# A hybrid decoder trunk: the spread inverse softmax sums in another buffer ring, and one small transpose in another PSUM bank

## The chip, the cores and the metric

The kernel runs on one core of one Trainium2 chip. The metric is the device time of one execution in microseconds (us); the median of three runs before the change is 1223.66 us (1223.54 to 1223.89). In the profile the engines are PE (TensorE, matrix products), PEld (its weight loads), DVE (VectorE), ACT (ScalarE), POOL (GpSimd) and SP (SyncE, which issues all transfers of this kernel, in order).

## The reference

Two layers over a sequence of 1024 tokens of width 1024. Each projects its input, runs a main branch and a memory attention, gates both, projects back and normalises. The main branch of the second layer is a forgetting attention with 16 heads of width 64, and the change lies there:

```python
logits = jnp.einsum('bqhd,bkhd->bhqk', qi, k) * scale
logits = logits + (ci[..., :, None] - cum_k[:, :, None, :])
logits = jnp.where(mask[None, None], logits, -jnp.inf)
p = jax.nn.softmax(logits, axis=-1)
return jnp.einsum('bhqk,bkhd->bqhd', p.astype(v.dtype), v)
...
y = jnp.concatenate([y_main * jax.nn.silu(g_main), y_mem * jax.nn.silu(g_mem)], axis=-1)
return y @ w_out
```

The kernel does not divide by the softmax's sums at once. It multiplies the unnormalised probabilities by the values and divides the output of a pair of heads afterwards, by a product with the inverse sums.

## The kernel before

**Heads and pairs.** The function `fox` runs over the 16 heads, two to a pair (`pr` is 0 to 7, `b` is 0 or 1 within it), and for each head over eight row blocks of 128 queries (step `i`, from the longest block, 1024 keys, to the shortest, 128). A last, shorter round (`hd == HEADS`) finishes what is left. Into these steps it mixes dense projections (`slab`, L253), which are to keep PE busy: keys, queries, values and gates of later pairs, and at the end the first part of the output projection (L498).

**One row block.** In `probs`, POOL writes the causal mask into the forget row R (`affine_select`, L881). It can do so only when DVE has read R for the block before. PE makes the logits in one of three banks "L" (L231). DVE adds R and finds the row's extreme (L889), for long blocks in two parts; the second part contains the masked columns. ACT takes the exponentials into one of two banks "T" and adds up their sums (L895), then writes their high half as float16 into a buffer of the ring "P" (L902). DVE writes the low half beside it (`halves`, L909), one step later. `turn` transposes the buffer by a transfer (L941), after which the buffer is free again. Five steps later (`LAG`) PE multiplies with the values (L958, L964) into the single bank "O", and ACT and DVE move the result out (L970, L971), which frees that bank.

**The inverse sums of a pair.** They are made in the round after the pair's second head, so those of pair `pr - 1` while pair `pr` runs; "in pair 6" below means then. At step 2 `inverse_rows` adds and inverts the sums on DVE, PE turns them with one small transpose (L920) into bank "O", ACT copies the result (L921), and SP writes it to DRAM (L922). At step 3 `inverse_wide` takes a buffer of 128x1024 and loads each head's inverse sums into 64 of its partitions (L944; in the last round L929). `pair_out` multiplies the pair's output by it in four pieces on POOL (L981). For most pairs POOL multiplies each piece with the gate as well (L983); pairs 3, 5 and 6 get their gate later, in `late_gate`. Then the output goes to DRAM (`y1d`, L985). The output projection reads `y1d` back (L529), splits it into a high and a low part (L187 on ACT, L188 on DVE) and multiplies (L498).

**Rings.** A ring is a number of equal buffers under one name; a new tile takes one whose former owner is done, and its first writer waits for that. "P" has four buffers. The probabilities of a row block use them, and before the change the spread inverse sums too; later the norm's two vectors (L517) and part of one output weight do. "V" has four: the turned values of a pair, and in the last pair and after it the high and low parts of two output weights (numbers 1 and 9 of `wtags`, L1092).

**What sets the order.** PE's instructions stand in the order in which the code writes them. The other engines' orders are set by a scheduler when the kernel is built, and each engine runs its own in order. One that waits holds everything behind it on its engine.

Of the kernel before, what the change touches and what calls it, by code (L numbers as in the profile page):

```python
# [9 lines left out]
F32 = mybir.dt.float32  # L10
# [8 lines left out]
P = 128  # L19
S = 1024  # L20
D = 1024
KT = D // P
ST = S // P
NH = 512
# [75 lines left out]
def trunk_kernel(ctx, tc, x, xT, memT, win, wk, wv0, wv, wmk, wmv, wout, poolw, pscale, lng, lnb, bforget, out):  # L100
# [21 lines left out]
    def nm(tag):  # L122
        count[0] += 1
        return f"{tag}{count[0]}"

    def sb(shape, tag, bufs, dt=F32, where=None):
        return (where or pool).tile(shape, dt, tag=tag, name=nm(tag), bufs=bufs)

    def ps(shape, tag, bufs):
        return psum.tile(shape, F32, tag=tag, name=nm(tag), bufs=bufs)  # L130
# [554 lines left out]
    with tc.tile_pool(name="in1", bufs=1) as in1:  # L685
# [7 lines left out]
        def vt(shape, dt=F32R):  # L693
            return sb(shape, "V", 4, dt, in1)
# [219 lines left out]
        def inverse_rows(pr, sums, rows):  # L914

            r = sums[:, 0]
            nc.vector.tensor_tensor(r, sums[:, 0], sums[:, 1], ALU.add)
            nc.vector.reciprocal(r, r)
            t = ps([P, NH], "O", 1)[: 2 * ST, :P]
            nc.tensor.transpose(t, r.rearrange("p b i -> p (b i)"), ident)  # L920
            nc.scalar.copy(rows, t)  # L921
            nc.sync.dma_start(inverses[pr], rows)  # L922

        def inverse_wide(pr):

            wide = sb([P, S], "P", 4)
            for b in range(2):
                load = wide[64 * b : 64 * b + 64], inverses[pr, ST * b : ST * b + ST].rearrange("i q -> (i q)").partition_broadcast(64)
                due.append(load) if pr < 7 else nc.sync.dma_start(*load)  # L929
            return wide  # L930
# [70 lines left out]
        def fox(following, out_proj):  # L1001
# [8 lines left out]
            for hd in range(HEADS + 1):  # L1010
# [22 lines left out]
                for i in range(ST if hd < HEADS else LAG):  # L1033
# [35 lines left out]
                    if hd and b == 0 and i == 2:  # L1069
                        if hd == HEADS:  # L1070
                            inverse_rows(pr - 1, sums, G()[: 2 * ST, :P])
                        else:
                            inverse_rows(pr - 1, past_sums, o[: 2 * ST, :P])
                    if hd and b == 0 and i == 3:
                        inv = inverse_wide(pr - 1)
# [86 lines left out]
```

## Time and profile before

| | |
|---|---|
| median of three runs | 1223.66 us |
| the profiled execution | 1221.92 us |
| its span, first to last instruction | 1220.2 us |
| mean granted TensorE clock | 0.995 |
| share of the span in which PE, DVE, ACT, POOL are busy | 97, 61, 49, 19% |

The forgetting attention lies between about 654 us (the first L902) and 1106.7 us (the last write to `y1d`), the output projection and the norms behind it. A row of the timeline reads: start in us, duration in us, engine, line, operation, what it writes `<-` what it reads, shape, count; in brackets how long the engine had stood idle before it and what ended that. A row of the waits reads: who waited, `<-` for what, us in total, times, the longest. A row of the chain that ended last reads: start, duration, what. A row of the windows reads: from:to, its length, then the busy time of PE, PEld, DVE, ACT and POOL with their instructions, then the granted clock of PE (1.00 is full speed), the mean busy share of the 16 DMA engines and GB/s.

### The profile page before, as it was taken

What the parts mean: (1) busy time and instruction counts of PE and PEld (TensorE: products, weight loads), DVE (VectorE), ACT (ScalarE), POOL (GpSimd) and SP (SyncE); (2) the same over time, 40 slices, a digit from 0 to 9 for tenths busy, and PEclk for the clock granted to TensorE, in tenths of its full rate; (3) what the DMA queues carried; (4) which work ended last, traced back from release to release, by engine and by line L of the source; (5) the groups of instructions that cost most, each with busy time, mean ns of one, the idle gap of its engine ahead of it and who ended that gap; (6) DMA issues with size and microseconds to landing.
All of it is one profiled execution on the core that took longest, in us unless ns stands there. A gap on an engine that the chain in (4) does not pass through costs nothing.

```text
span 1220.2 us, 19470 instructions
## 1 busy us (share of the span) xinstructions
PE 1188.5 (97%) x6910; PEld 752.9 (62%) x7026; DVE 749.2 (61%) x1621; ACT 595.0 (49%) x1326; POOL 228.6 (19%) x352
## 2 busy tenths in 40 slices
PE   9999999999999999999999999999999999989997
PEld 4567665555556568567776666666666656655554
DVE  6544776375644478257455767576666867664644
ACT  6433654262521125257235667566666767582110
POOL 2000000000000013000013344434444325522000
PEclk9999999999999999999999999999999999999999
DMA  6333554242453336234438787889879799985431
GB/s 234 118 101 91 123 114 155 79 129 85 141 191 114 109 104 197 73 82 106 152 80 195 167 182 182 198 154 212 187 178 191 191 200 217 231 238 171 171 105 52
DMA packets 268947, 182.91 MB, mean 150 GB/s; under 512 B 212657, under 2 KB 226225, under 8 KB 268849
## 3 DMA queue, kind: packets, MB, share of 16 engines
q1 hardware_dynamic: 268848, 181.66, 57.2%
q8 instruction: 55, 0.90, 0.3%
q14 instruction: 44, 0.35, 0.1%
HBM read 99.17 MB, written 22.68 MB: 100 GB/s over the span
## 4 chain that ended last, share of the span: by engine, by line
PE 77%; DVE 6%; ACT 5%; issue 5%; DMA 4%; POOL 2%; SPq 0%; DVEq 0%; POOLq 0%; ACTq 0%
PE pj L253 42%; PE L L231 8%; PE L L498 8%; PE pj L498 6%; PE O L498 2%; DVE MK L889 2%; ACT T L895 2%; PE T L498 2%; DMA P<-inverses 2%; PE L L750 2%; PE pj L231 2%; ACT P L902 2%; DVE P L909 2%; PE T L231 1%; PE O L958 1%
## 5 line engine op out<-in xcount | busy, mean ns | idle before, releaser
L253 PE MATMUL pj<-A,w 128*128 128x512 f32 (+1 forms) x1894 | 606.3, 401 | 2.6 <-ACT A L187 0.5
L253 PE MATMUL pj<-A,wl 128*128 128x512 bf16 x945 | 358.1, 380 | 3.9 <-issue 0.5
L253 PEld LDWEIGHTS pj<-A,w 128*128 128x128 f32 x976 | 182.7, 191 | 47.4 <-ACT A L187 1.7
L253 PEld LDWEIGHTS <-w 128*128 128x128 bf16 x992 | 95.9, 98 | 123.4 <-issue 35.9
L895 ACT ACTIVATE T<-MK,s 128x512 f32<-128x512 f32 x192 | 111.2, 579 | 105.7 <-DVE s L889 103.1
L909 DVE SCALAR_TENSOR_TENSOR P<-T,P 128x512 f16<-128x512 f32 x192 | 104.6, 554 | 84.6 <-ACT P L902 83.3
L253 PEld LDWEIGHTS <-wl 128*128 128x128 bf16 x992 | 97.7, 98 | 94.2 <-issue 6.2
L498 PEld LDWEIGHTS <-T 128*128 128x128 bf16 x736 | 70.7, 98 | 86.3 <-issue 4.4
L188 DVE TENSOR_TENSOR wl<-raw,w 128x512 bf16<-128x512 f32 x98 | 72.0, 739 | 84.2 <-ACT w L187 82.3
L231 PE MATMUL L<-B,B 128*128 128x512 f32 (+3 forms) x384 | 108.5, 387 | 8.8 <-DVE s L889 8.8
L187 ACT CAST w<-raw 128x512 fp32r<-128x512 f32 x106 | 64.8, 618 | 97.2 <-PE pj L253 69.7
L192 POOL TENSOR_SCALAR A<-A 128x512 bf16<-128x512 f32 (+1 forms) x20 | 16.9, 859 | 434.2 <-ACT A L187 434.2
L902 ACT ACTIVATE P<-T 128x512 f16<-128x512 f32 x192 | 87.2, 482 | 10.8 <-POOL G L981 6.8
L231 PEld LDWEIGHTS L<-B,B 128*128 128x128 f32 x384 | 71.3, 189 | 32.5 <-DVE s L889 12.3
L889 DVE CUSTOM_DVE_ANT_0 MK<-L,R 128x512 f32<-128x512 f32 (+3 forms) x128 | 72.6, 567 | 15.5 <-PE L L231 7.6
L881 POOL TENSOR_SCALAR_AFFINE_SELECT R<-R 128x128 f32<-128x128 f32 x128 | 41.2, 327 | 196.8 <-DVE s L889 181.9
L187 ACT CAST T<-T 128x1024 fp32r<-128x1024 f32 x23 | 24.1, 1046 | 103.4 <-DMA T<-y1d 56.2
L198 POOL TENSOR_TENSOR wl<-raw,w 128x512 bf16<-128x512 f32 x54 | 69.1, 1280 | 4.1
L188 DVE TENSOR_TENSOR T<-T,T 128x1024 bf16<-128x1024 f32 x23 | 28.1, 1221 | 48.7 <-ACT T L187 28.8
L197 POOL TENSOR_SCALAR w<-raw 128x512 fp32r<-128x512 f32 x54 | 35.8, 663 | 61.6 <-DMA B<-B 47.3
L498 PE MATMUL L<-B,T 128*128 128x512 bf16 (+1 forms) x165 | 43.2, 390 | 0.2
L889 DVE CUSTOM_DVE_ANT_0 MK<-L,R,s 128x512 f32<-128x512 f32 (+1 forms) x64 | 37.2, 581 | 7.2 <-POOL R L881 3.4
(267 smaller groups left out, 1725.8 us busy)
## 6 DMA issues: line engine op xcount, KB each, us to landing
raw<-in_win_dram SPq DMA_DIRECT2D x96, 256.0 KB, 2.9
raw<-in_wout_dram SPq DMA_DIRECT2D x40, 256.0 KB, 2.7
B<-B SPq DMA_DIRECT2D x32, 256.0 KB, 4.4
R<-cumd SPq DMA_DIRECT2D x16, 512.0 KB, 4.7
y0d<-Y SPq DMA_DIRECT2D x12, 512.0 KB, 3.1
T<-y0d SPq DMA_DIRECT2D x12, 512.0 KB, 4.1
T<-y1d SPq DMA_DIRECT2D x11, 512.0 KB, 5.0
raw<-in_wmk_dram SPq DMA_DIRECT2D x16, 256.0 KB, 2.6
```

Of the source, the lines that this page charges most:

```text
L187: pin(nc.scalar.copy(hi, src))
L188: pin(by.tensor_tensor(lo[0], src, hi.bitcast(F32), ALU.subtract))
L197: nc.gpsimd.tensor_scalar(hi, src, 1.0, 1.0, ALU.mult, ALU.mult)
L198: nc.gpsimd.tensor_tensor(lo[0], src, hi.bitcast(F32), ALU.subtract)
L231: nc.tensor.matmul(acc, a, b, start=i == 0, stop=i == len(terms) - 1)
L253: nc.tensor.matmul(acc, a, b, start=start, stop=stop)
L498: nc.tensor.matmul(acc, y, w, start=c == 2 and j == firsts[id(acc)], stop=c == 1 and j == lasts[id(acc)])
L881: nc.gpsimd.affine_select(R[:, qs], R[:, qs], [[-1, P]], ALU.is_ge, -NEG, base=0, channel_multiplier=1).ins
L889: nc.vector.tensor_tensor_reduce(p[:, lo:up], lg, R[:, lo:up], 1.0, top, ALU.add, ALU.min, m[:, n : n + 1])
L895: nc.scalar.activation(e, p[:, lo:up], AF.Exp, bias=top, scale=-1.0, accum_out=sums[:, n, hd % 2, i : i + 1],)
L902: nc.scalar.activation(pair[:, lo:up], e, AF.Copy, scale=PSCALE)
L909: nc.vector.scalar_tensor_tensor(pair[:, L + lo : L + up], e, PSCALE, pair[:, lo:up], ALU.mult, ALU.subtract)
```

## The change

```diff
@@ inverse_rows
-            t = ps([P, NH], "O", 1)[: 2 * ST, :P]
+            t = ps([P, NH], *(("O", 1) if pr < 7 else ("T", 2)))[: 2 * ST, :P]
             nc.tensor.transpose(t, r.rearrange("p b i -> p (b i)"), ident)
@@ inverse_wide
-            wide = sb([P, S], "P", 4)
+            wide = vt([P, S], F32)
```

`vt` takes a buffer of ring "V". The spread inverse sums of all eight pairs move there, and the small transpose of the last pair goes into one of the two "T" banks. No instruction is added or removed. The orders of all engines are as before up to the last round; what differs before that is what an instruction waits for.

On ACT in pair 6 (`L902` writes the high half of a row block into ring P; `DMAHW` are transfers, `Pool` is POOL):

```order
 L895 ACTIVATE T_10857,sums_10576<-MK_10847,s_10851 128x384 [waits DVE_49]
-L902 ACTIVATE P_10859<-T_10857 128x384 [waits DMAHW5_49,Activation_49]
+L902 ACTIVATE P_10859<-T_10857 128x384 [waits DMAHW4_49,Activation_49]
 L799 COPY B_10601<-pj_10744 64x512 [waits DVE_49]
 L895 ACTIVATE T_10901,sums_10576<-MK_10891,s_10895 128x256 [waits DVE_49]
-L902 ACTIVATE P_10903<-T_10901 128x256 [waits DMAHW6_49,DMAHW2_49,DMAHW7_49,Activation_49,Pool_49]
+L902 ACTIVATE P_10903<-T_10901 128x256 [waits DMAHW5_49,Activation_49]
 L895 ACTIVATE T_10930,sums_10576<-MK_10920,s_10924 128x128 [waits DVE_49]
```

The second L902 no longer waits for POOL and for the loads of the sums; it waits for one earlier transfer only.

On PE in the last round, around the small transpose:

```order
 L498 LDWEIGHTS B_11812
 L498 MATMUL L_12123<-MK_11696,B_11812 128x512 [waits Pool_49]
-L920 MATMUL O_12210<-ident,sums_11297 16x128 [waits DVE_49]
+L920 MATMUL T_12210<-ident,sums_11297 16x128 [waits Activation_49]
 L498 LDWEIGHTS B_11811
 L498 MATMUL L_12124<-V_11617,B_11811 128x512
```

Its place is the same; it waits for ACT's reading of an earlier exponentials' tile in place of DVE's reading of bank O.

On ACT in the last round (`V_12332` and `V_12333` are the high and low parts of output weight 9, `G_11296` is pair 7's output, `T_12429` the high part of an output that is read back):

```order
 L187 COPY T_12429<-T_12428 128x1024
-L187 COPY V_12332<-raw_12330 128x512
-L187 COPY V_12332<-raw_12337 128x512
 L187 COPY P_12344<-raw_12342 128x512
 L194 COPY G_12345<-P_12344 128x512
 L970 ACTIVATE G_11296<-O_12237,unscale 64x512
-L194 COPY V_12333<-V_12332 128x512 x2
+L187 COPY V_12332<-raw_12330 128x512
+L187 COPY V_12332<-raw_12337 128x512
 L187 COPY P_12344<-raw_12349 128x512
 L194 COPY G_12345<-P_12344 128x512
 L187 COPY B_12356<-raw_12354 128x512
```

The splits of output weight 9 stand behind the last evacuation of the values (L970), and its low part later still. On DVE the same splits move behind L971 in the same way, and on SP one of the norm's vectors (L517) is loaded ahead of a weight load.

## The prediction

> **What bounds the kernel now.** I read the page first, then the waits by engine, then the timeline of TensorE (PE) at each of its waits, then the chain that ended last, and last the windows with the granted clock.
>
> ```profile
> PE 1188.5 (97%) x6910; PEld 752.9 (62%) x7026; DVE 749.2 (61%) x1621; ACT 595.0 (49%) x1326; POOL 228.6 (19%) x352
> PE L L231 <- DVE s L889: 8.8, 8, 2.1
> PE O L920 <- DVE G L971: 3.1, 1, 3.1
> PE L L498 <- ACT T L187: 1.4, 1, 1.4
> ACT P L902 <- POOL G L981: 6.8, 5, 4.7
> ```
>
> PE is busy 97% of the span, so time can only come out of PE's few waits: 8.8 us for logit banks (L231), 3.1 for the O bank at the last transpose (L920), 1.4 near the end (L498). The last row is what the first edit removes: ACT waits 6.8 us in five places for a buffer of P's ring that the spread inverse sums hold until POOL's last product (L981). Whether PE feels that is to be seen pair by pair.
>
> ```profile
> 727.71 0.50 PE L231 MATMUL L<-B,B 128*128 128x256 f32 x2 [1.10 <-DVE s L889]
> 838.80 0.50 PE L231 MATMUL L<-B,B 128*128 128x256 f32 x2 [2.08 <-DVE s L889]
> 948.70 0.57 PE L231 MATMUL L<-B,B 128*128 128x256 f32 x2 [1.93 <-DVE s L889]
> 995.38 0.62 PE L231 MATMUL L<-B,B 128*128 128x384 f32 x2 [0.41 <-DVE s L889]
> 1000.89 0.50 PE L231 MATMUL L<-B,B 128*128 128x256 f32 x2 [1.83 <-DVE s L889]
> ```
>
> These are PE's waits shortly after an inverse product, in pairs 1, 3, 5 and 6 (two). The two kinds of pair differ.
>
> **Pair 6: the ring is the cause, -2.24 us.**
>
> ```profile
> 987.11 0.54 POOL L881 TENSOR_SCALAR_AFFINE_SELECT R<-R 128x128 f32<-128x128 f32 x2 [1.43 <-DVE s L889]
> 987.57 0.20 ACT L895 ACTIVATION_READ_ACCUMULATOR T<-MK,s 128x1 f32 x1
> 989.69 2.79 POOL L981 TENSOR_TENSOR G<-G,P 128x256 f32<-128x256 f32 x4 [2.05 <-DMA P<-inverses]
> 992.51 0.38 ACT L902 ACTIVATE P<-T 128x256 f16<-128x256 f32 x1 [4.74 <-POOL G L981]
> 992.93 0.42 DVE L909 SCALAR_TENSOR_TENSOR P<-T,P 128x256 f16<-128x256 f32 x1 [4.70 <-ACT P L902]
> 1000.16 0.67 DVE L889 CUSTOM_DVE_ANT_0 MK<-L,R 128x512 f32<-128x512 f32 x1
> ```
>
> ACT is ready at 987.77 and stands until 992.51, when L981 frees the buffer. DVE stands behind it in order, frees its logit banks late, and PE meets the last of this at 1000.89 (L889 at 1000.16 frees the bank). POOL had made the two masks that DVE needs next (L881) already at 987.11, ahead of L981. With the sums in V, L902 needs only a P buffer whose transpose was issued before 983; ACT and DVE run some 4.7 us earlier, more than the 0.41 and 1.83 that PE waits. I take both: -2.24. Ends: -2.24, and 0 if something else holds DVE.
>
> **Pairs 1, 3 and 5: the ring is not the cause, 0 us.** Pair 3 stands for the three:
>
> ```profile
> 831.67 1.43 POOL L983 TENSOR_TENSOR G<-G,G 128x256 f32<-128x256 f32 x2
> 831.75 0.28 ACT L902 ACTIVATE P<-T 128x128 f16<-128x128 f32 x1 [0.55 <-POOL G L981]
> 833.04 0.30 POOL L881 TENSOR_SCALAR_AFFINE_SELECT R<-R 128x128 f32<-128x128 f32 x1
> 833.38 0.75 DVE L889 CUSTOM_DVE_ANT_0 MK<-L,R,s 128x512 f32<-128x512 f32 x1 [0.42 <-POOL R L881]
> ```
>
> Here POOL's order puts L981 and L983 ahead of the mask that the next head's first row block needs. ACT's L902 waits only 0.55 for the ring, but the next L889 waits for that mask until 833.38 whatever ACT does, and PE's 2.08 hangs on this L889. The edit moves neither POOL's work nor the load that starts it. I take 0. The gain's far end, were the ring the cause after all, is the three waits, 1.10 + 2.08 + 1.93 = 5.11, and what hangs on them (below). Pairs 2 and 4 are not among these: the five waits make 7.35 of the 8.8, and the other three of the eight share 1.45.
>
> **The last transpose: PE's 3.06 us go, and come back at the end of the chain, 0 us.**
>
> ```profile
> 1085.10 0.62 ACT L187 CAST w<-raw 128x512 fp32r<-128x512 f32 x1 [1.48 <-DMA raw<-in_wout_dram]
> 1087.29 0.28 PE L920 MATMUL O<-ident,sums 128*16 128x128 f32 x1 [3.06 <-DVE G L971]
> 1090.52 0.25 ACT L921 COPY G<-O 16x128 f32<-16x128 f32 x1
> 1093.72 5.85 DMA P<-inverses
> 1103.88 1.43 POOL L981 TENSOR_TENSOR G<-G,P 128x256 f32<-128x256 f32 x2
> 1106.74 3.39 DMA y1d<-G
> 1110.21 4.97 DMA T<-y1d
> 1115.25 1.04 ACT L187 CAST T<-T 128x1024 fp32r<-128x1024 f32 x1 [12.75 <-DMA T<-y1d]
> 1116.35 0.73 PE L498 MATMUL L<-R,T 128*128 128x512 f32 x2 [1.41 <-ACT T L187]
> ```
>
> In the exponentials' bank L920 no longer waits for DVE's L971, so PE goes on at 1084.23. But L921, the copy behind it on ACT, runs at 1090.52, three us after the transpose, because ACT works through weight copies in order from 1085.10, where it waited for a load. None of these waits for PE. From L921 a chain of transfers and POOL products ends at ACT's L187 at 1115.25 and PE's product with pair 7's output, for which PE already waits 1.41. PE comes there 3.06 earlier and waits 4.47. I take 0 at the end; ends: 0 and -3.06.
>
> The loads of the sums (L929) land after 5.85 us, beside two weight loads; in the changed order one of those stands behind DVE's later split. The nearest rows of the same transfer in the chain:
>
> ```profile
> 822.93 4.21 DMA P<-inverses
> 983.29 6.26 DMA P<-inverses
> ```
>
> I take 5.35, some way back to the quieter row: -0.5. Ends: 4.21 gives -1.64, 6.26 gives +0.41. The wait becomes 3.97.
>
> V's ring adds a wait at the end: the second of the two V buffers of output weight 9 is the one the sums hold, so its splits on DVE and ACT wait for the fourth L981, at 1105.31, with weight 11's and then pair 7's output queued behind. Four splits of about 0.7 end near 1108, before pair 7's output comes at 1115.25: 0 us. The cover is ACT's idle 12.75; past it, each us would count.
>
> **The clock: +1.5 us.** PE's granted clock (the figure after the busy times) answers to such waits:
>
> ```profile
> 836.35:839.76 3.41, 1.33 (x7) 0.78 (x6) 3.24 (x8) 1.17 (x3) 0.15 (x1) 1.00 0.59 160
> 839.76:843.17 3.41, 3.41 (x9) 2.67 (x9) 1.92 (x6) 3.08 (x8) 0.44 (x2) 0.50 0.86 246
> 843.17:846.58 3.41, 3.41 (x18) 2.08 (x18) 3.21 (x9) 3.07 (x10) 0.59 (x2) 1.00 1.01 268
> 945.58:948.99 3.41, 1.48 (x8) 0.79 (x6) 2.71 (x6) 1.66 (x4) 0.00 (x0) 1.00 0.39 120
> 948.99:952.40 3.41, 3.41 (x10) 2.48 (x10) 1.92 (x6) 2.89 (x7) 0.29 (x1) 0.50 1.13 256
> 1085.51:1088.93 3.42, 1.64 (x9) 0.80 (x10) 1.81 (x3) 3.37 (x6) 0.00 (x0) 1.00 0.91 252
> 1088.93:1092.34 3.41, 3.41 (x24) 1.79 (x22) 3.02 (x5) 3.41 (x9) 0.00 (x0) 1.00 0.93 327
> ```
>
> After the waits of 2.08 and 1.93 the clock is 0.50 for 3.41 us: 9 matmuls run there, 18 in the next stretch of the same length, so each fall costs 1.7. The falls start 109.23 apart, 32 times 3.41, so the clock is set on a fixed grid of such windows. A window with 1.78 idle (1085.51) brought no fall; one with 1.93 (945.58) did. Each execution may start elsewhere on the grid. A wait of 3.97 lying anywhere on it leaves at least 1.98 idle in one window, so the clock falls nearly always, and after 1116 PE runs to its end with no wait left to absorb it. A fall that comes when PE runs again costs 1.7; one inside the wait costs only the rest of its window, 0.8 to 1.4; where two windows are mostly idle, 2.4. Over all positions that is an estimate of +1.5; ends 0 and +2.5. The wait of 3.06 that goes could lower the clock too, elsewhere on the grid, but PE's 1.41 at 1116.35 then covered most of the loss.
>
> **Sum.** -2.24 + 0 + 0 - 0.5 + 1.5 = -1.24. The profiled execution took 1221.92 (span 1220.2); the median of the runs is 1223.66, 1.74 above it, which I carry unchanged: **1222.4 us**.
>
> **Rivals.**
>
> *The clock stays up.* If only a fully idle window lets it fall, a wait of 3.97 holds one in (3.97 - 3.41) / 3.41 = 16% of positions; otherwise the sum is -2.74, 1220.9. Against it stand the two falls after windows with 1.33 and 1.48 us of work. The Trainium skill states this rule (TensorE: Matmul & The Clock Gate, "What's actually happening": half clock after at least one idle window of about 3.4 us, on a free-running window); the trace agrees on length and grid but not on "idle". Chance 0.20.
>
> *The ring held pairs 1, 3 and 5 too.* If ACT's 0.55 reached PE in each, 1.65 would go, and the waits of 2.08 and 1.93 would shrink to 1.53 and 1.38, under the 1.78 that brought no fall: 3.4 more. -1.24 - 1.65 - 3.4 = -6.29, 1217.4. For it: the ACT row at 831.75. Against: the mask at 833.04. Chance 0.12.
>
> *Slower: the end's transfers do not come earlier with PE.* DMA is full just before:
>
> ```profile
> 1001.00:1041.00 40.00, 39.67 (x256) 26.54 (x262) 30.55 (x77) 29.74 (x73) 17.52 (x27) 1.00 1.00 222
> ```
>
> Its share is 1.00. If the loads before 1085.10 come when they came, the chain from L921 stays put, pair 6's 2.24 only lengthens the wait, to 6.7, and the clock's cost (1.6 over all positions of a wait of 6.7) and the landing's +0.41 remain: 1225.7, up to 1227.5 with two slow windows. The time ends above that of before once the chain gains less than 1.0 of the 2.24 (1.5 - 0.5). Against it: PE waits for no load between 1001 and 1074, and the loads are issued as DVE frees buffers, in PE's pace. Chance 0.17.
>
> **How the numbers follow.** Forecast 0.46, the rivals 0.20, 0.12 and 0.17, anything else 0.05. The forecast's own range is 1220.6 to 1224.2 (clock 0.8 with the landing's -1.64, clock 2.4 with its +0.41). For 8 in 10 I reach over the clock's rival and most of the slower one: 1218.5 to 1226.0. A measurement here tells about 0.2% (2.45 us) from no change. Faster by more: 0.17 of the first rival, all of the second, 0.02 of the rest, 0.31. Slower by more: 0.10 of the third and 0.03, 0.13. Within: 0.56.
>
> **What would show it.** Right: no ACT wait on L981 at L902; no PE wait near 995 and 1000 while those near 727, 838 and 948 stay; L920 without a wait; PE's wait for pair 7's output at about 4 us, followed by a stretch at clock 0.50. Wrong: the waits in pairs 1, 3, 5 shrink; L921 moves closer to L920; the final wait is short; DVE or ACT still holds weight splits when pair 7's output lands.

## The result, and the profile after

| | before | after |
|---|---|---|
| median, 6 runs each, same chip | 1222.67 us (1220.62 to 1223.89) | 1218.63 us (1217.81 to 1219.23) |
| ratio, 95% interval | | 0.9969 (0.9956 to 0.9981) |
| profiled execution | 1221.92 us (span 1220.2) | 1218.30 us (span 1216.6) |
| mean granted clock of it | 0.995 | 0.996 |

The medians lie 4.0 us apart; by the ratio the kernel is 0.31% faster. A second batch of runs on another occasion gave 0.9968 (0.9955 to 0.9980). The forecast was 1222.4 us within a range of 1218.5 to 1226.0, that is 1.24 us faster; the direction was right and the size too small.

The waits by engine after the change (who waited, for what, us in total, times, longest):

```profile
PE L L231 <- DVE s L889: 7.8, 6, 2.1
PE L L498 <- ACT T L187: 3.8, 1, 3.8
ACT P L902 <- DMA T<-P: 3.1, 4, 1.4
```

ACT's wait for POOL's L981 is gone from the list; what is left at L902 is for the transposes out of P (3.1 us, before 1.3). PE's largest row is only 1.0 us shorter: the 2.24 of pair 6 are out of it, but pair 1's wait is 0.88 longer in this execution. PE's wait for bank O at L920 is gone too, and the wait near the end has grown from 1.4 to 3.8. The timeline of PE tells which waits are left:

```profile
729.28 0.51 PE L231 MATMUL L<-B,B 128*128 128x256 f32 x2 [1.98 <-DVE s L889]
840.43 0.50 PE L231 MATMUL L<-B,B 128*128 128x256 f32 x2 [2.09 <-DVE s L889]
950.41 0.79 PE L231 MATMUL L<-B,B 128*128 128x256 f32 x2 [2.03 <-DVE s L889]
1112.73 0.73 PE L498 MATMUL L<-R,T 128*128 128x512 f32 x2 [3.75 <-ACT T L187]
```

The three waits in pairs 1, 3 and 5 stand; the two of pair 6 (0.41 and 1.83 before) are not there. The chain behind the last transpose after the change, from ACT's copy to the split of pair 7's output:

```profile
1087.27 0.25 ACT L921 COPY G<-T 16x128 f32<-16x128 f32 x1
1090.85 4.87 DMA V<-inverses
1102.42 4.72 DMA y1d<-G
1107.21 4.34 DMA T<-y1d
1111.63 1.04 ACT L187 CAST T<-T 128x1024 fp32r<-128x1024 f32 x1 [8.21 <-DMA T<-y1d]
```

From L921 to PE's product it takes 1112.73 - 1087.27 = 25.46 us, before 1116.35 - 1090.52 = 25.83. L920 itself runs at 1081.32, but L921 6.0 us behind it, because ACT still works through weight copies in order. The windows of the clock's grid (from:to, length, then busy time of PE, PEld, DVE, ACT, POOL, the granted clock, DMA share, GB/s), first at pair 3, then around the final wait:

```profile
837.82:841.23 3.41, 1.32 (x8) 0.71 (x7) 3.23 (x8) 1.17 (x3) 0.00 (x0) 1.00 0.59 169
841.23:844.64 3.41, 3.41 (x10) 2.64 (x9) 1.92 (x6) 3.08 (x8) 0.50 (x2) 0.50 0.94 265
...
1107.47:1110.89 3.42, 1.50 (x7) 0.49 (x5) 0.00 (x0) 0.00 (x0) 0.00 (x0) 1.00 0.76 254
1110.89:1114.30 3.41, 1.57 (x7) 1.31 (x8) 1.23 (x1) 1.04 (x1) 0.00 (x0) 1.00 0.98 342
1114.30:1117.71 3.41, 3.36 (x16) 2.22 (x16) 1.23 (x1) 1.56 (x2) 0.00 (x0) 1.00 0.20 71
```

Behind pair 3's wait the clock falls to 0.50 for one window, as it did before. Behind the final wait it does not: the border at 1110.89 cuts the 3.75 us almost in the middle, 1.91 idle on one side and 1.84 on the other.

**Where the time came from.** PE's 6910 matmuls stand in the same order before and after the change, so the start of one and the same matmul can be compared between two executions, counted from the first matmul of each. The table shows how much later or earlier than in the profiled execution of before PE came through each stretch (stretches by the times of before; each number is the difference of two starts at the end of a stretch minus the same difference at its beginning; minus means earlier). The first column holds what executions differ in by chance at the start and by the falls behind pairs 3 and 5, and in the last two rows the gain of the later products; the kernels below the first two rows are those of the experiments.

| execution | to 990 us | pair 6, 990 to 1003 | pair 7, 1003 to 1080 | end, 1080 to 1120 | falls of the clock behind pairs 3 and 5, final wait |
|---|---|---|---|---|---|
| after | +1.69 | -2.79 | -1.56 | -0.98 | 2, 0 |
| after, second execution | -2.60 | -2.79 | -0.37 | +0.69 | 0, 1 |
| first edit alone | -2.73 | -2.51 | -0.56 | -0.68 | 0, 0 |
| second edit alone | -0.83 | +0.65 | +0.09 | +1.60 | 1, 1 |
| V in pair 6 only | +0.62 | -2.43 | +3.50 | +1.19 | 1, 1 (and one in pair 7) |
| V in pairs 6 and 7 | -0.58 | -2.80 | -1.55 | +1.76 | 1, 1 (two windows long) |
| V in all but pair 7 | -0.60 | -2.79 | -1.56 | +1.34 | 1, 1 (two windows long) |
| later products | -11.73 | -2.81 | -0.40 | +1.51 | 0, 1 |
| later products, bank O | -11.62 | -2.40 | -0.70 | -1.51 | 0, 0 |

Pair 6 gives 2.4 to 2.8 us wherever its sums are in V. In the one kernel of the table that keeps them in P, the second edit alone, it gives nothing and comes out 0.65 later. That is the core of the result. The other columns are what the experiments are about.

### The profile page after: what moved, and what is told of

The parts are those of the page before. It is cut to its first block, busy times and chain, and to the rows that moved or that the text cites. A ratio compares the mean times of both kernels' runs of the same rounds, so it can differ in the third digit from the quotient of the medians.

```text
span 1216.6 us, 19471 instructions
## 1 busy us (share of the span) xinstructions
PE 1185.8 (97%) x6910; PEld 752.7 (62%) x7026; DVE 750.8 (62%) x1621; ACT 594.8 (49%) x1326; POOL 228.7 (19%) x352
## 4 chain that ended last, share of the span: by engine, by line
PE 81%; DVE 5%; ACT 4%; issue 4%; DMA 4%; POOL 2%; SPq 0%; POOLq 0%; DVEq 0%; ACTq 0%
PE pj L253 44%; PE L L231 9%; PE L L498 8%; PE pj L498 6%; PE O L498 2%; PE T L498 2%; PE L L750 2%; ACT T L895 2%; DVE MK L889 2%; PE pj L231 2%; PE O L958 2%; DVE P L909 1%; PE T L231 1%; ACT P L902 1%; DMA V<-inverses 1%
## 5 line engine op out<-in xcount | busy, mean ns | idle before, releaser
L498 PEld LDWEIGHTS <-T 128*128 128x128 bf16 x736 | 70.7, 98 | 86.4 <-issue 4.4
L902 ACT ACTIVATE P<-T 128x512 f16<-128x512 f32 x192 | 87.3, 482 | 5.8 <-DMA T<-P 3.1
L889 DVE CUSTOM_DVE_ANT_0 MK<-L,R 128x512 f32<-128x512 f32 (+3 forms) x128 | 72.6, 567 | 14.9 <-POOL R L881 8.1
L498 PE MATMUL L<-B,T 128*128 128x512 bf16 (+1 forms) x165 | 43.3, 390 | 0.2
L889 DVE CUSTOM_DVE_ANT_0 MK<-L,R,s 128x512 f32<-128x512 f32 (+1 forms) x64 | 37.1, 580 | 7.8 <-POOL R L881 3.1
```

The costliest lines, as they stand in the source:

```text
L498: nc.tensor.matmul(acc, y, w, start=c == 2 and j == firsts[id(acc)], stop=c == 1 and j == lasts[id(acc)])
L889: nc.vector.tensor_tensor_reduce(p[:, lo:up], lg, R[:, lo:up], 1.0, top, ALU.add, ALU.min, m[:, n : n + 1])
L902: nc.scalar.activation(pair[:, lo:up], e, AF.Copy, scale=PSCALE)
```

## The experiments

Twelve experiments were run, one of them with the changed kernel itself. Each stands against runs of the kernel before that were taken in the same batch (medians 1221.47, 1221.32 and 1222.21 us); the ratios are to those.

| kernel | median us (runs) | ratio | 95% interval |
|---|---|---|---|
| first edit alone | 1216.93 (5) | 0.9958 | 0.9943 to 0.9972 |
| second edit alone | 1221.35 (12) | 0.9997 | 0.9987 to 1.0008 |
| V in pair 6 only | 1221.12 (12) | 0.9987 | 0.9975 to 0.9999 |
| after, again | 1217.94 (7) | 0.9968 | 0.9955 to 0.9980 |
| V in pairs 6 and 7 | 1219.19 (12) | 0.9977 | 0.9967 to 0.9986 |
| V in all but pair 7 | 1218.68 (10) | 0.9974 | 0.9961 to 0.9988 |
| later products | 1209.36 (5) | 0.9898 | 0.9882 to 0.9915 |
| later products, bank O | 1207.42 (5) | 0.9886 | 0.9868 to 0.9903 |
| filled final wait | 1218.37 (12) | 0.9970 | 0.9958 to 0.9982 |
| exchanged parts | 1214.35 (6) | 0.9942 | 0.9930 to 0.9954 |
| later products, exchanged parts | 1206.27 (4) | 0.9874 | 0.9857 to 0.9891 |
| the same, bank O | 1206.56 (4) | 0.9878 | 0.9864 to 0.9893 |

### The two edits, each alone

```diff
 first edit alone
-            t = ps([P, NH], *(("O", 1) if pr < 7 else ("T", 2)))[: 2 * ST, :P]
+            t = ps([P, NH], "O", 1)[: 2 * ST, :P]
 second edit alone
-            wide = vt([P, S], F32)
+            wide = sb([P, S], "P", 4)
```

> Only the first edit: the spread inverse sums in V for all pairs, the last transpose in bank O as before. Theory A (the end is set by the chain behind L921, so the transpose's wait is only moved into the final wait): within 0.6 us of the changed kernel, 1218.6 to 1219.2; PE waits about 3.1 at L920 and 0.7 to 1.4 for pair 7's output, together the 3.75 of the changed kernel. Theory B (the bank's 3.06 us reach the end): about 3 us slower than the changed kernel, 1221.7. In both, PE's waits of 0.41 and 1.83 in pair 6 are gone.

> Only the second edit: the last transpose in an exponentials' bank, the sums in P as before. Theory A: the time of before within 0.7 us, 1222.0 to 1223.3; no wait at L920, a final wait of about 4.4; PE's waits of 0.41 and 1.83 in pair 6 stand. Theory B: 3 us faster than before, about 1219.7, with a final wait of 1.4.

The diff is against the changed kernel: each of the two takes one edit back. The first edit alone takes 1216.93 us, the second alone 1221.35, against 1221.47 before. The whole gain is in the ring. The first edit alone is 1.0 us faster than the changed kernel in the same batch (1217.94), where agreement within 0.6 was expected; their intervals overlap. The timeline of PE at the end of the first edit alone:

```profile
1080.45 0.28 PE L920 MATMUL O<-ident,sums 128*16 128x128 f32 x1 [1.34 <-DVE G L971]
1085.86 0.72 PE L958 MATMUL O<-T,V 128*128 128x128 f16 x10 [0.82 <-ACT G L921]
1109.90 0.73 PE L498 MATMUL L<-R,T 128*128 128x512 f32 x2 [0.85 <-ACT T L187]
```

With bank O PE waits three times: for the bank before L920 (1.34, where about 3.1 was expected), for it again at L958, since the copy L921 frees it late (not foreseen), and for pair 7's output. Together that is 3.01 us, where the two executions of the changed kernel have one wait of 3.75 and 3.08. The bank moves PE's idle time about and removes none of it, as Theory A has it. In the second edit alone the waits of pair 6 stand (1.04 and 1.83), with the same cause as before, and the end has the long wait:

```profile
992.33 0.38 ACT L902 ACTIVATE P<-T 128x256 f16<-128x256 f32 x1 [3.98 <-POOL G L981]
1000.72 0.50 PE L231 MATMUL L<-B,B 128*128 128x256 f32 x2 [1.83 <-DVE s L889]
1116.27 1.02 PE L498 MATMUL L<-R,T 128*128 128x512 f32 x2 [3.96 <-ACT T L187]
```

Theory B, by which the bank's 3 us reach the end, falls with both kernels.

### Which pairs carry the gain

```diff
 V in pair 6 only
-            wide = vt([P, S], F32)
+            wide = vt([P, S], F32) if pr == 5 else sb([P, S], "P", 4)
 V in pairs 6 and 7: pr in (5, 6)
 V in all but pair 7: pr != 6
```

> The sums are in V only for the inverses that are used in pair 6, in P for all others; the last transpose in an exponentials' bank. Theory C (pair 7's two short waits of 0.41 and 0.60 went because ACT and DVE come out of pair 6 earlier, or by chance): the changed kernel's time within 0.5 us, 1218.1 to 1219.1, and no wait of PE at its L231 in pair 7. Theory D (they went because pair 7's own product left P's ring): 1.0 to 1.6 us slower than the changed kernel, 1219.6 to 1220.2, ACT's L902 waits for POOL's L981 in pair 7, and PE's two waits of 0.4 to 0.6 are back there. In both, pair 6 has no wait of PE, and waits in pairs 1, 3 and 5 are about 2 us each.

> The sums are in V only for the inverses used in pairs 6 and 7, in P for all others; the last transpose in an exponentials' bank. Theory E (pairs 6 and 7 carry the whole gain, ACT's waits of 0.55 in pairs 1, 3 and 5 reach nothing): the changed kernel's time within 0.7 us, 1217.3 to 1218.7. Theory F (the ring costs something in pairs 1 to 5 too, by the waits or by falls of the clock that hang on them): 1.5 us or more slower than the changed kernel, 1219.5 or more, with the waits in pairs 3 and 5 longer than 2.1 or followed by falls more often.

> The sums are in V for all pairs but for those used in pair 7, which stay in P; the last transpose in an exponentials' bank. Theory D (pair 7's own product belongs out of P's ring: with it there, POOL's products of the late gates, and DVE's masks behind them, come later): 1 to 3 us slower than the changed kernel, 1219 to 1221, with a PE wait for a weight copy (L498 behind ACT's L187) of 0.6 to 1.8 near 1076 and often a fall of the clock behind it. Theory C (pair 7's gain was chance): the changed kernel's time within 0.7 us. In both, pair 6 has no wait.

V in pairs 6 and 7 gives 0.9977, and its interval overlaps that of the changed kernel. With P in pairs 1, 3 and 5 ACT's wait for L981 is there (1.9 us in four places), and PE's waits near 839 and 948 are 2.10 and 1.85, no longer than in the executions with V there (2.01 to 2.14, and 1.80 to 2.10). The clock fell once behind them, against twice, once or not at all in those. The time does not decide: 1219.19 lies above Theory E's 1217.3 to 1218.7 and below Theory F's 1219.5. The waits speak for Theory E. That the ring costs nothing in pairs 1 to 5 is thus not shown to better than about 1 us, the difference of the two ratios.

V in all but pair 7 gives 0.9974, and PE gains the same 1.56 us in pair 7 as with V there. So pair 7's gain does not need pair 7's own sums to be in V; Theory D falls, Theory C stands in the part that says so. V in pair 6 only contradicts both. It is 3.2 us slower than the changed kernel in the same batch and loses 3.5 us in pair 7 in its profiled execution, which was also its slowest (its runs lie between 1217.45 and 1224.75). There POOL, DVE and PE read:

```profile
1065.05 1.41 POOL L998 TENSOR_TENSOR R<-R,G 128x256 f32<-128x256 f32 x2 [7.94 <-DMA R<-y1d]
1066.74 0.48 DVE L889 CUSTOM_DVE_ANT_0 MK<-L,R,s 128x256 f32<-128x256 f32 x1 [3.41 <-POOL R L881]
1076.53 0.55 PE L498 MATMUL L<-MK,B 128*128 128x512 f32 x1 [1.83 <-ACT B L187]
```

In the kernel before, DVE and PE read at these places, with a first short wait of PE ahead of them:

```profile
1055.95 0.50 PE L231 MATMUL L<-B,B 128*128 128x256 f32 x2 [0.41 <-DVE s L889]
1066.64 0.48 DVE L889 CUSTOM_DVE_ANT_0 MK<-L,R,s 128x256 f32<-128x256 f32 x1 [1.93 <-POOL R L881]
1076.42 0.50 PE L498 MATMUL L<-MK,B 128*128 128x512 f32 x1 [0.60 <-ACT B L187]
```

With V in pair 6 only POOL waits for the load of an output that gets its gate late, the next mask stands behind its product in order, DVE's L889 behind the mask, ACT's weight copies behind that, and PE last. Behind the wait of 1.83 the clock falls once, and at 1.7 us for a fall that is about half of the 3.5 us. The changed kernel has the same chain, with a DVE wait of 0.19 at that place in its first execution and 1.83 in its second, and PE waits of 0 and 0.51. All 14 profiled executions fit together here: where DVE waits under 0.9 us for this mask PE hardly waits at L498 (0.03 at most), and where DVE waits 1.55 us or more PE waits about 1.3 us less than DVE (1.6 less with V in pair 6 only). So PE's second wait in pair 7 hangs on when POOL gets to this mask, in this kernel on when the load lands. Why the load lands late in this execution, and why this kernel's runs are slower than those of V in all but pair 7, which has the same ring in pair 7, stays open.

### The changed kernel again

> The changed kernel once more, for a second profiled execution. Time 1218.6 within 0.6. If the clock's grid lies by chance against the waits, and a window with about 2 us of idle suffices for a fall, a final wait of about 3.75 is followed by 0.50 for 3.41 us here in most executions (about 1 us longer than one without); if such a wait at this place never lowers the clock, it stays at 1.00 behind it as in the first one, and the execution takes 1218.3 within 0.5. The falls behind pairs 3 and 5 lie on a grid of 3.41 us in both cases.

The median is 1217.94 us, at the edge of what was expected, and the clock fell behind the final wait this time:

```profile
1106.74:1110.15 3.41, 0.44 (x2) 0.40 (x3) 0.46 (x1) 1.04 (x1) 0.00 (x0) 1.00 0.93 294
1110.15:1113.56 3.41, 3.41 (x10) 2.66 (x9) 0.76 (x1) 1.03 (x1) 0.00 (x0) 0.50 0.81 281
1113.56:1116.97 3.41, 3.36 (x15) 1.93 (x16) 1.23 (x1) 2.10 (x3) 0.00 (x0) 1.00 0.00 0
```

Here one window held nearly the whole wait, and 10 matmuls ran in the window behind it where 15 run in the next. Behind pairs 3 and 5, after waits of 2.07 and 1.85, there was no fall in this execution. The same waits are followed by a fall or not as the grid lies. With one fall where the first execution has two, this one took 1216.86 us.

### POOL's order in pairs 1, 3 and 5

```diff
         def pair_out(pr, o, g, inv):
-            yield
+            late = g is not None and pr < 7
+            for _ in range(5 if late else 1):
+                yield
             for k in (3, 2, 1, 0):
                 cols = slice(k * 2 * P, (k + 1) * 2 * P)
-                nc.gpsimd.tensor_tensor(o[:, cols], o[:, cols], inv[:, cols], ALU.mult)
+                with tc.issue_after(masked[-1]) if late else nullcontext():
+                    nc.gpsimd.tensor_tensor(o[:, cols], o[:, cols], inv[:, cols], ALU.mult)
...
-                run(finished)
+                if b or hd == HEADS or gs.get(pr - 1) is None:
+                    run(finished)
```

> The changed kernel, with POOL's products of pairs that have their gate at hand (L981 and L983 of its numbering) put behind the masks: they are spread over the second head's steps 1 to 4, each behind the mask of its step. Theory G (POOL's order sets PE's waits in pairs 1, 3 and 5): the waits of about 2 us near 728, 840 and 950 fall below 0.6, and with them the clock's falls behind pairs 3 and 5; 4.5 to 6 us of waits and 0 to 3.4 of clock, so 4.5 to 9 us faster than the changed kernel, 1209 to 1213.5. Theory H (the waits come from the handing over of the two heads itself, the mask only came last): they stay above 1.2 each, and the time is within 2 us of the changed kernel's.

> The same as the run before, but with the last transpose in bank O as before the change (the first edit and the later products). Theory A (the bank is worth nothing): the time of the run before within 0.8 us, the sum of PE's waits from L920 on as long as its final wait there, within 0.8. Theory B (it is worth up to 3 us): 2 to 3 us slower than that run.

1209.36 us, 8.6 us faster than the changed kernel (0.9898 against 0.9968). Theory G holds. In the two profiled executions PE, DVE and ACT run the same instructions in the same order; only POOL's order differs, and that of some transfers. In the changed kernel POOL and DVE read, in pair 3:

```profile
828.89 1.44 POOL L981 TENSOR_TENSOR G<-G,V 128x256 f32<-128x256 f32 x2 [1.86 <-DMA V<-inverses]
830.28 1.43 POOL L983 TENSOR_TENSOR G<-G,G 128x256 f32<-128x256 f32 x2
831.66 0.29 POOL L881 TENSOR_SCALAR_AFFINE_SELECT R<-R 128x128 f32<-128x128 f32 x1
...
831.99 0.29 DVE L889 CUSTOM_DVE_ANT_0 MK<-L,R 128x128 f32<-128x128 f32 x1 [1.49 <-POOL R L881]
835.00 0.75 DVE L889 CUSTOM_DVE_ANT_0 MK<-L,R,s 128x512 f32<-128x512 f32 x1 [0.94 <-POOL R L881]
```

DVE waits twice for a mask behind products. In the kernel with later products each mask runs at once when DVE has let go of R, and the products (L984 and L986 there) follow in the gaps:

```profile
822.74 0.54 POOL L881 TENSOR_SCALAR_AFFINE_SELECT R<-R 128x128 f32<-128x128 f32 x2 [1.95 <-DVE s L889]
827.25 0.29 POOL L881 TENSOR_SCALAR_AFFINE_SELECT R<-R 128x128 f32<-128x128 f32 x1 [3.97 <-DVE s L889]
827.51 0.73 POOL L984 TENSOR_TENSOR G<-G,V 128x256 f32<-128x256 f32 x1
828.32 0.74 POOL L986 TENSOR_TENSOR G<-G,G 128x256 f32<-128x256 f32 x1
832.66 0.29 POOL L881 TENSOR_SCALAR_AFFINE_SELECT R<-R 128x128 f32<-128x128 f32 x1 [3.60 <-DVE s L889]
```

Its PE waits 0.4 us in all behind L889, where the changed kernel waits 7.8, and no fall of the clock is left before the final wait. With bank O it takes 1207.42 us. The expected agreement within 0.8 us failed, on the other side than Theory B has it: the exponentials' bank is 1.9 us slower, as it is 1.0 slower in the changed kernel. In both comparisons the intervals overlap, so neither is shown alone. The profiles say what may lie behind it: the one long wait of 4.55 is followed by a window at 0.50, the two waits of 1.73 and 1.27 with bank O are not.

### The clock alone

```diff
+                for _ in range(3 if self.l and (sp, c) == (0, 1) else 0):
+                    nc.tensor.matmul(accs[0][0][0][:64], ident[:64, 64:], gb[1][:64, :NH], start=False, stop=False)
                 for n, _ in enumerate(self.closing(accs[sp], kept) if at_end else self.products(accs[sp], c, yh, yl)):
```

> The changed kernel with three products of a zero block of the identity with the norm's vector ahead of PE's product with pair 7's output; they add zero to its bank and keep PE busy for about 2.6 us of the final wait. Theory I (the long final wait lowers the clock in most executions and that costs about 1.5 us): no fall of the clock behind the final wait, and 0.8 to 1.7 us faster than the changed kernel, about 1217. Theory J (the clock's fall there costs nothing that counts): the changed kernel's time, or up to 0.5 slower.

The products ran for 2.79 us (six passes), PE's final wait was cut to 1.68, and the clock fell all the same:

```profile
1109.97:1113.38 3.41, 1.73 (x6) 0.62 (x5) 0.59 (x1) 1.04 (x1) 0.00 (x0) 1.00 1.04 371
1113.38:1116.79 3.41, 3.41 (x10) 2.64 (x9) 1.86 (x2) 1.08 (x2) 0.00 (x0) 0.50 0.29 104
```

With 1218.37 us nothing was gained. Since the fall that was to be prevented came, the run does not price it; it decides for neither theory. It does show that 1.73 us of PE's time in a window, in part with a quarter of the array, did not hold the clock up.

### The end with the chain covered

```diff
-                accs[0], order = self.accs, [(0, 0), (1, 2), (0, 1), (1, 0), (1, 1)]
+                accs[0], order = self.accs, [(0, 0), (1, 2), (1, 0), (0, 1), (1, 1)]
```

> The changed kernel, with the order of two parts of the output projection exchanged: the products of the second 256 rows with the first four pairs' outputs (48 matmuls, about 10 us) come ahead of those of the first 256 rows with pair 7's half. Theory A (the chain behind L921 sets the end, and absorbs what the bank saves): PE waits less than 0.5 for pair 7's output, no fall of the clock there, 3.7 to 5.4 us faster than the changed kernel, 1212.8 to 1214.6. Theory K (another transfer or split takes its place, such as the load of the second rows' outputs): less than 2 us faster, with a wait of PE for that load.

> The kernel with the later products and the last transpose in an exponentials' bank, with the same exchange. Theory A: its final wait of 4.55 and the fall behind it go, 4.5 to 6.2 us faster than without the exchange, 1203.2 to 1204.9. Theory K: less than 2 us faster.

> The kernel with the later products and the last transpose in bank O, with the same exchange. Theory A: its final wait of 1.27 goes, the wait at L920 of 1.3 to 1.7 stays, so 1.2 to 1.5 us faster than without the exchange, about 1206, and 1.3 to 3 us slower than the run before: with the chain covered, the exponentials' bank is worth its wait. If the bank is worth nothing even then, the two differ by less than 0.8.

The changed kernel with the exchange takes 1214.35 us, inside the expected 1212.8 to 1214.6; by the ratios, 0.9942 against 0.9968, it gains 3.2 us, a little less than the 3.7 expected. The final wait is gone, as Theory A has it, and in its place stand two short waits for the outputs that are now read first.

```profile
1107.47 0.39 PE L498 MATMUL T<-B,T 128*128 128x512 bf16 x1 [0.50 <-ACT T L187]
1108.73 0.82 PE L498 MATMUL T<-B,T 128*128 128x512 bf16 x3 [0.87 <-DVE T L188]
```

With the later products the exchange gives less than expected with the exponentials' bank (1206.27, where 1203.2 to 1204.9 stood) and about what was expected with bank O (1206.56). The reason is the same load, which now comes 1.29 late:

```profile
1098.58 0.39 PE L498 MATMUL T<-B,T 128*128 128x512 bf16 x1 [1.29 <-ACT T L187]
1099.84 0.39 PE L498 MATMUL T<-B,T 128*128 128x512 bf16 x1 [0.87 <-DVE T L188]
```

These two are 2.16 us of waits with the exponentials' bank, against 1.39 and 0.68 at L920 and L958 with bank O. Even where pair 7's chain is covered, the two banks come out alike. The expected 1.3 to 3 us between them did not come.

The fastest kernels, 1206.3 to 1207.4 us, are three whose intervals overlap; all leave before and after the change behind by some 15 and 11 us.

## Why the prediction was too small

Of the 3.8 us between the forecast time and the median after, 1.0 is the starting point: the forecast started from the median of three runs, 1223.66, and the six runs of the comparison have 1222.67. The rest is the gain, 1.24 against 4.0 by the medians (3.8 by the ratio).

**Pair 6: right, and somewhat undersized.** The forecast took PE's two waits, 2.24. PE gains 2.79 in that stretch in both executions of the changed kernel and 2.40 to 2.81 in the other kernels with V. At each of the two places PE comes forward by some 0.27 more than the idle time that the profile counts (0.69 and 2.10, for waits of 0.41 and 1.83).

**Pairs 1, 3 and 5: right.** 0 was forecast; the waits stand at 1.98, 2.09 and 2.03. That they hang on POOL's order, which was read from the mask at 833.04, is shown by the later products, which remove them. The rival that put the ring there (1217.4) lies nearer to the measured time than the forecast, but for another reason.

**The last transpose: right.** The saving of 3.06 comes back in the final wait, which is 3.75 and 3.08 in the two executions (forecast 3.97), and each edit alone shows it.

**The landing: near in sum, by luck.** -0.5 was forecast for the chain from L921, -0.37 came in the first execution and -1.37 in the second (24.46 us). In the profiled executions without the exchange the chain takes 24.3 to 26.5 us, so the term is smaller than what executions differ by. Its parts moved otherwise: in the first execution the loads of the sums took 4.87 where 5.35 was assumed, and the write and the read behind them took most of the rest back. Weight 9's splits on ACT and DVE lay under the wait, as forecast.

**Pair 7: missing from the sum.** 0.37 and 1.56 us came there in the two executions, -0.4 to -1.6. The prediction had counted only waits right behind an inverse product and had passed over 0.41 and 0.60 in pair 7. PE gains there in every kernel with V in pair 6 but one, also where pair 7 itself keeps P. The second of the two waits hangs on POOL's mask, as shown above; how V in the earlier pairs brings that mask forward is not shown.

**The clock: this term failed.** +1.5 rested on the step that a wait of 3.97 "lying anywhere on it leaves at least 1.98 idle in one window, so the clock falls nearly always". In the changed kernel's own execution it was 3.75, split 1.91 and 1.84, and no fall came. So the fall comes often, but not "nearly always" by the reason given: 1.91 idle in one window was not enough. As to the end alone the step was not bad: with the exponentials' bank the clock fell behind the final wait in six of the seven executions in the table, and the five others with that bank and V lose 0.69 to 1.76 in the last stretch where the forecast had +1.0. What it left out, or put at nothing for the wait of 3.06, is the other side. Waits that the change removes may have lowered the clock too. Waits of 1.84 to 1.93 at pair 5 did so in some executions; behind those of pair 6 and L920 no profiled execution shows a fall. And whether a fall comes behind pairs 3 and 5 differs from one execution to the next, while the single profiled execution of before was taken as if its two falls were all. Over all runs the mean granted clock is 0.9955 after (13 runs) and 0.9952 before (63 runs): 0.0003 of some 1218 is a saving of 0.4 us, and by the scatter of the runs that is uncertain by about 1 us either way. So a cost of 1.5 us is not borne out, and a saving is not shown. The rival with the clock up (1220.9) lies nearer to the measured time than the forecast, but its rule does not hold: the clock fell behind windows with up to 1.73 us of work.

With these in place the sum is -2.8 for pair 6, about -1.0 for pair 7 (the mean of the two executions), -0.4 to -1.4 for the chain and between -0.4 and nothing for the clock, -4.2 to -5.6 us. The ratios of the two batches give -3.8 (0.0031 of 1222.67) and -3.9 (0.0032 of 1221.47). The difference is within what executions differ by, 1 us and more in each of the last three terms.

## What to carry to other kernels

A wait on the busiest engine is removed only where its whole chain is followed: here the ring held ACT in five places, but only in one did nothing else, such as a mask behind products in POOL's order, end later. Where a saving lies ahead of a wait that a chain of transfers ends, it moves into that wait; look for other work to put there instead, which brought about 3 us to the changed kernel here where the bank brought none. When waits near the clock's limit are common, take the expected number of falls from several executions of both kernels, not from one profile.

## What was unexpected in the hardware

The falls of the clock lie on a grid of 3.41 us in all executions, and one lasts one window, or two where the wait goes on in the window behind it. What decides a fall is roughly half a window. In all 14 profiled executions, apart from the first 11 us, each window with less than 1.47 us of PE's time was followed by one, of those with 1.47 to 1.73 some were and some were not, and after a window at full clock with more there was none. Two rows at the same pair 5, in the kernel with the second edit alone and in the one with V in pairs 6 and 7, with the window behind each:

```profile
945.87:949.28 3.41, 1.47 (x7) 0.67 (x5) 2.55 (x5) 1.97 (x5) 0.00 (x0) 1.00 0.35 120
949.28:952.69 3.41, 3.39 (x16) 2.77 (x17) 1.78 (x5) 2.59 (x7) 0.29 (x1) 1.00 1.17 252
```

```profile
945.03:948.44 3.41, 1.56 (x9) 0.82 (x7) 2.78 (x6) 1.60 (x3) 0.00 (x0) 1.00 0.39 113
948.44:951.85 3.41, 3.41 (x11) 2.46 (x10) 1.92 (x6) 2.92 (x7) 0.29 (x1) 0.50 1.16 265
```

The first had less work and kept its clock, so PE's busy time is not exactly what is measured. The Trainium skill (TensorE: Matmul & The Clock Gate, "What's actually happening") speaks of at least one idle window. No window before the falls inside the kernel was idle as a whole: the emptiest had 0.16 us of work, in the kernel with V in pair 6 only, and most had between 1.2 and 1.6. The measurement decides.
